# Opening a decoder layer with x0 loaded first, modulation per single input block, and sums of squares by column groups on TensorE

## The chip, the cores and the metric

The kernel runs on one core of one Trainium2 chip. The metric is device time in microseconds (us) of one execution, which covers the span of the profile and the little that lies around it. Smaller is better.

## What is computed

One inference step of a hybrid decoder layer for 1024 prompt tokens and 8 short sample sequences of 8 tokens (64 rows), model width 2048, all in float32. What matters here:

```python
def rmsnorm(x, g):
    xf = x.astype(jnp.float32)
    y = xf * lax.rsqrt(jnp.mean(xf * xf, axis=-1, keepdims=True) + EPS)
    return y.astype(x.dtype) * g
...
    mod = jax.nn.silu(c) @ w_ada + b_ada            # (9, 2048) @ (2048, 6144)
    shift, scale, gate = jnp.split(mod[:, None, :], 3, axis=-1)
    xn = rmsnorm(x, norm_g) * (1.0 + scale) + shift
    z = xn @ w_in                                    # 5120 columns
...                                                  # three mixers, two of them with a layernorm
    out = jnp.concatenate([ya, yb, yc], axis=-1) @ w_out
    return x + gate * out, ...                       # then a final rmsnorm
```

So before the first column of `z` can be summed over the 2048 input channels, the kernel needs the root mean square of every token (a sum over all channels) and, for each block of 128 channels, its shift and scale, which are two blocks of columns of a 2048-deep product with `w_ada`.

## The kernel before

Channels lie on the 128 partitions, tokens on the free axis. The width 2048 is 16 blocks of 128 (`KT` = 16). Tokens go through in two parts: T0 = 512 prompt tokens, then T1 = 576 (the other 512 and the 64 sample rows). Every large product is made of three matmuls: activations and weights are split into a high and a low part (`xn_hi`, `xn_lo`, `w_hi`, `w_lo`), and `mm3` (L131 to L133) adds hi·hi, hi·lo and lo·hi in PSUM. ScalarE makes `w_hi` (L97), VectorE makes `w_lo` (L98), per loaded weight tile.

The change concerns the **opening**, which is everything until the first product of T0 stands. It holds three kinds of work, all fed by DMAs that SyncE issues in one queue:
- the modulation: `w_ada` for shift and scale, 64 blocks of 512 KB, an odd block as one DMA into a tile of the pool tag `ar` (L689) and an even one as two DMAs of 256 KB into spare `xn_hi`/`xn_lo` tiles (L694). `ada_mm` (L142) multiplies with `silu(c)` (`cz`, 32 columns wide with padding), so that four such matmuls write four groups of 32 PSUM partitions. A **unit** in the kernel before is 8 blocks: four column blocks (shift and scale of two input blocks) over all of the depth. `ada_fin` copies the result to SBUF (ScalarE, `rows`, L168), transposes it on TensorE (L169) and adds bias and norm weight on VectorE into `adam` (L173, L178).
- the tokens: 16 loads of `x0` (L658), squares on ScalarE (L662, L665), two running sums `acc0` on VectorE (L666), then `rstd_of`: matmuls with a 128-column piece of the sum as weights and the one column of `one_d` as moving operand (`ps_var`, L210), a reciprocal square root with one Newton step on the few resulting columns (`rstd_cols`, L188 to L194), and `row_bcast` (`ps_bc`, L201), which spreads it over all partitions for R0 (L717).
- the first six column blocks of `w_in` (`ps_g`): `k_step(k)` loads `wi_g[k]` (384 KB, three buffers), splits it, and issues 6 x 3 matmuls of 512 columns. It needs `xn[k]` from `norm_x` (L225 to L227), and so `adam` of block k and R0.

The loop of the opening has nine turns: turn i multiplies unit i (8 blocks) and, one turn behind, runs `norm_pair(i - 1)` and two `k_step`s. Units 0 and 1 come before the first `k_step`, with all x0 loads in the middle of unit 0.

`rstd_of` and `row_bcast` are also used by the four layernorms, by the sums of squares of the second part's tokens (`stats_x1`), and by the three final normalisations, the last of which ends the kernel.

The code is written once in program order; a scheduler with priorities (`tc.high_priority`) then fixes the order of instructions on each engine, and each engine runs its list in that order.

Of the kernel before, what the change touches and what calls it, by code (L numbers as in the profile page):

```python
# [44 lines left out]
def decoder_layer(ctx: ExitStack, tc: tile.TileContext, a):  # L45
# [21 lines left out]
    with tc.high_priority(10 * HP):  # L67
        nc.sync.dma_start(cT, a["cT"])
# [817 lines left out]
```

## Time and profile before

| | us |
|---|---|
| median of three runs | 1513.63 (1512.84 to 1514.2) |
| the profiled execution | 1511.97 |
| its span in the profile | 1510.3 |
| opening, up to the first matmul of `ps_s` | 137.0 |
| TensorE busy in the span | 1469.2 (97%) |
| VectorE busy | 923.8 (61%) |
| ScalarE busy | 597.7 (40%) |

The rows below come from that one profiled execution, which lies 1.7 us under the median. PE is TensorE's matmul stream, PEld its weight loads, DVE is VectorE, ACT ScalarE, POOL GpSimd, SP SyncE. Starts are counted from the span's start. A float32 matmul appears as two instructions. Matmul durations overlap (the next one starts before the last has drained), so the pace of TensorE is read from starts. The idle time in brackets, with an arrow, tells what ended it.

### The profile page before, as it was taken

To read this page: it belongs to the slowest core of one execution; us is meant where nothing else is said; L and a number is where in the kernel's file an instruction comes from. 1 tells how busy PE (TensorE), PEld (TensorE's weight loads), DVE (VectorE), ACT (ScalarE), POOL (GpSimd) and SP (SyncE) were. 2 spreads that over 40 slices of the span, in tenths; PEclk is the share of its full clock that TensorE was granted. 3 is DMA by queue.
4 is the path that set the end of the run, shared out by engine and by line. 5 is a ranking of instruction groups with operands and counts; after the bars stand their busy time and mean duration, and the time that the engine had idled before them with its cause. 6 is when DMAs were issued, how large, how long until landed. Compare 5 with 4: busy or idle time off the path is not lost.

```text
span 1510.3 us, 25287 instructions
## 1 busy us (share of the span) xinstructions
PE 1469.2 (97%) x10072; PEld 1320.9 (87%) x10072; DVE 923.8 (61%) x1760; ACT 597.7 (40%) x1006; POOL 48.6 (3%) x120
## 2 busy tenths in 40 slices
PE   4999999999999999999999999999999999999996
PEld 3777888887777778888999999999999999999996
DVE  4436993679467452554885995387956744334345
ACT  4225422264557442433533422235445753222220
POOL 0000000010000000000000000011100000000000
PEclk9999999999999999999999999999999999999998
DMA  9995233334444543564573222222222221244323
GB/s 365 411 367 183 81 102 98 98 98 145 159 162 149 163 152 103 168 201 149 157 240 105 76 74 91 81 84 86 94 88 71 70 80 59 81 132 124 107 79 126
DMA packets 86550, 206.10 MB, mean 136 GB/s; under 512 B 10656, under 2 KB 26656, under 8 KB 86432
## 3 DMA queue, kind: packets, MB, share of 16 engines
q1 hardware_dynamic: 85280, 203.30, 41.3%
q8 instruction: 79, 1.29, 0.3%
q10 hardware_dynamic: 1152, 1.18, 0.2%
q14 instruction: 39, 0.32, 0.1%
HBM read 194.70 MB, written 9.74 MB: 135 GB/s over the span
## 4 chain that ended last, share of the span: by engine, by line
PE 92%; DMA 4%; DVE 2%; ACT 1%; issue 1%; SPq 0%; DVEq 0%; ACTq 0%
PE ps_s L131 23%; PE ps_s L132 23%; PE ps_s L133 22%; PE ps_g L133 6%; PE ps_g L131 6%; PE ps_g L132 6%; PE ps_ada L146 2%; DMA a_raw<-w_ada 2%; DMA w_raw<-wi_g 1%; PE ps_bc L201 1%; DMA x<-x 1%; PE ps_gate L131 1%; PE ps_var L210 1%; DVE w_lo L98 1%; PE ps_gate L132 0%
## 5 line engine op out<-in xcount | busy, mean ns | idle before, releaser
L98 DVE TENSOR_TENSOR w_lo<-w_raw,w_hi 128x512 fp32r<-128x512 f32 (+1 forms) x480 | 311.3, 653 | 407.6 <-PE ps_s L133 266.8
L131 PE MATMUL ps_s<-xn_hi,w_hi 128*128 128x288 f32 (+1 forms) x1632 | 538.4, 330 | 1.8 <-ACT pad_a L421 1.6
L97 ACT CAST w_hi<-w_raw 128x512 fp32r<-128x512 f32 (+1 forms) x480 | 281.4, 592 | 651.2 <-PE ps_s L132 451.8
L132 PE MATMUL ps_s<-xn_lo,w_hi 128*128 128x288 f32 (+1 forms) x1632 | 534.6, 328 | 0.0
L133 PE MATMUL ps_s<-xn_hi,w_lo 128*128 128x288 f32 (+1 forms) x1632 | 532.5, 326 | 0.0
L131 PEld LDWEIGHTS ps_s<-xn_hi,w_hi 128*128 128x128 f32 x1632 | 306.0, 188 | 28.4 <-issue 2.8
L133 PEld LDWEIGHTS ps_s<-xn_hi,w_lo 128*128 128x128 f32 x1632 | 307.1, 188 | 22.0 <-issue 0.2
L132 PEld LDWEIGHTS ps_s<-xn_lo,w_hi 128*128 128x128 f32 x1632 | 306.5, 188 | 20.6 <-issue 0.5
L358 DVE SCALAR_TENSOR_TENSOR mx<-pad_b,vec,mx 128x512 f32<-128x512 f32 x240 | 177.6, 746 | 2.4
L131 PE MATMUL ps_s<-m_hi,w_hi 128*128 128x288 f32 (+1 forms) x480 | 157.1, 327 | 0.0
L132 PE MATMUL ps_s<-m_lo,w_hi 128*128 128x288 f32 (+1 forms) x480 | 156.6, 326 | 0.0
L133 PE MATMUL ps_s<-m_hi,w_lo 128*128 128x288 f32 (+1 forms) x480 | 156.5, 326 | 0.0
L131 PE MATMUL ps_g<-xn_hi,w_hi 128*128 128x288 f32 (+1 forms) x288 | 95.4, 331 | 0.7
L133 PEld LDWEIGHTS ps_s<-m_hi,w_lo 128*128 128x128 f32 x480 | 90.3, 188 | 6.2
L132 PEld LDWEIGHTS ps_s<-m_lo,w_hi 128*128 128x128 f32 x480 | 90.1, 188 | 6.2
L131 PEld LDWEIGHTS ps_s<-m_hi,w_hi 128*128 128x128 f32 x480 | 90.0, 187 | 6.2
L133 PE MATMUL ps_g<-xn_hi,w_lo 128*128 128x288 f32 (+1 forms) x288 | 93.5, 329 | 1.7 <-DVE w_lo L98 1.7
L131 PE MATMUL ps_g<-m_hi,w_hi 128*128 128x288 f32 (+1 forms) x288 | 94.2, 328 | 0.1
L132 PE MATMUL ps_g<-xn_lo,w_hi 128*128 128x288 f32 (+1 forms) x288 | 94.1, 327 | 0.0
L132 PE MATMUL ps_g<-m_lo,w_hi 128*128 128x288 f32 (+1 forms) x288 | 93.9, 326 | 0.0
L133 PE MATMUL ps_g<-m_hi,w_lo 128*128 128x288 f32 (+1 forms) x288 | 93.6, 326 | 0.0
L133 PEld LDWEIGHTS ps_g<-xn_hi,w_lo 128*128 128x128 f32 x288 | 54.2, 188 | 8.3 <-DVE w_lo L98 4.7
(200 smaller groups left out, 1462.8 us busy)
## 6 DMA issues: line engine op xcount, KB each, us to landing
w_raw<-wi_s SPq DMA_DIRECT2D x136, 512.0 KB, 3.5
w_raw<-wo_s SPq DMA_DIRECT2D x40, 512.0 KB, 3.5
a_raw<-w_ada SPq DMA_DIRECT2D x64, 256.0 KB, 6.8
a_raw<-w_ada SPq DMA_DIRECT2D x32, 512.0 KB, 6.9
g_raw<-w_ada SPq DMA_DIRECT2D x64, 256.0 KB, 2.9
w_raw<-wi_g SPq DMA_DIRECT2D x16, 384.0 KB, 7.1
w_raw<-wo_g SPq DMA_DIRECT2D x16, 384.0 KB, 3.0
w_raw<-wi_g SPq DMA_DIRECT2D x32, 192.0 KB, 2.5
```

The lines of the kernel that those rows point to most:

```text
L97: nc.scalar.copy(hi, raw)
L98: nc.vector.tensor_tensor(lo, raw, hi.bitcast(F32), op=ALU.subtract)
L131: nc.tensor.matmul(out, wh, xh, start=start, stop=False)
L132: nc.tensor.matmul(out, wh, xl, start=False, stop=False)
L133: nc.tensor.matmul(out, wl, xh, start=False, stop=stop)
L146: nc.tensor.matmul(pa[32 * j:32 * j + 32, 0:P], cz[:, k, :], raw[q][:, j * P:(j + 1) * P], start=(k == 0), stop=(k == KT - 1))
L201: nc.tensor.matmul(pb[:, c * w:(c + 1) * w], st[0:w, 1, c0 + c:c0 + c + 1].to_broadcast([w, P]), ident[0:w, 0:w], start=True, stop=True)
L210: nc.tensor.matmul(pv[0:w, c:c + 1], s[:, u + c * w:u + (c + 1) * w], ones[:, 0:1], start=(s is src[0]), stop=(s is src[-1]))
L358: nc.vector.scalar_tensor_tensor(out[:, :T0], pad[:, j:j + T0], w[:, j:j + 1], out[:, :T0], op0=ALU.mult, op1=ALU.add)
```

## The change

x0 comes first: its 16 loads stand ahead of `w_ada` (with one half block and the first 64 columns of `vec` between them), and `cT` moves to ScalarE's DMA queue. A unit of modulation becomes four blocks for **one** input block: the four groups of 32 partitions now hold shift and scale for two halves of the depth, and `ada_fin` adds the halves on VectorE. The opening has 16 turns: modulation of block i+1, then `norm_x(i)` and `k_step(i)`. Sums of squares are no longer added up on VectorE for x0; `var_mm` lets four matmuls with a 32-column weight of ones write four partition groups, each a quarter of the tokens, so the reciprocal square root works on rows of a quarter of the tokens (128, 144 or 72 columns) on all partitions, and `row_bcast` picks one partition per group. That form replaces the old one everywhere. The rest of `vec` (columns 64 on), and what is worked out from `lam` (`sw`, `sp8`), comes after the opening.

```diff
-        nc.sync.dma_start(cT, a["cT"])
+        nc.scalar.dma_start(cT, a["cT"])
...
-    def ada_mm(pa, b, raw):
+    def ada_mm(pa, raws, b, fine):
         for q in range(2):
-            k = 2 * b + q
+            t = 2 * b + q
             for j in range(4):
-                nc.tensor.matmul(pa[32 * j:32 * j + 32, 0:P], cz[:, k, :], raw[q][:, j * P:(j + 1) * P],
-                                 start=(k == 0), stop=(k == KT - 1))
+                k = 2 * t + j // 2 if fine else t
+                nc.tensor.matmul(pa[32 * j:32 * j + 32, 0:P], cz[:, k, :], raws[q][:, j * P:(j + 1) * P],
+                                 start=(t == 0), stop=(t == (7 if fine else 15)))
...
+    def ada_fin(k, pa):
+        pt = ada_turn(pa)
         with tc.high_priority(HP):
...
+            nc.vector.tensor_tensor(dst, pt[:, 0:2, :],
+                                    vec[:, o:o + 2].unsqueeze(2).to_broadcast([P, 2, 9]), op=ALU.add)
+            nc.vector.tensor_tensor(dst, dst, pt[:, 2:4, :], op=ALU.add)
...
+            nc.vector.tensor_scalar(sc, sc, 1.0, vec[:, o:o + 1], op0=ALU.add, op1=ALU.mult)
...
-    def row_bcast(st, c0, n):
+    def row_bcast(st, w, j0, n):
         pb = mi("ps_bc")
-        w = 96 if n % P else P
-        for c in range(n // w):
-            nc.tensor.matmul(pb[:, c * w:(c + 1) * w], st[0:w, 1, c0 + c:c0 + c + 1].to_broadcast([w, P]),
-                             ident[0:w, 0:w], start=True, stop=True)
+        for j in range(n):
+            nc.tensor.matmul(pb[:, j * w:(j + 1) * w], ident[:, 32 * (j0 + j):32 * (j0 + j) + 1].to_broadcast([P, P]),
+                             st[:, 1, 0:w], start=True, stop=True)
         return pb
+
+    def var_mm(pv, s, u, w, ones, start, stop):
+        for j in range(4):
+            nc.tensor.matmul(pv[32 * j:32 * j + 32, 0:w], ones.to_broadcast([P, 32]), s[:, u + j * w:u + (j + 1) * w],
+                             start=start, stop=stop)
...
-            acc = acc0[k % 2]
-            if k < 2:
-                nc.scalar.activation(acc, x[:, :T0], AF.Square)
-            else:
-                sq = sp_.tile([P, TM], F32, tag="xr", name="x_sq")
-                nc.scalar.activation(sq[:, :T0], x[:, :T0], AF.Square)
-                nc.vector.tensor_tensor(acc, acc, sq[:, :T0], op=ALU.add)
...
+            sq = sp_.tile([P, TM], F32, tag="xr", name="x_sq")
+            nc.scalar.activation(sq[:, :T0], x[:, :T0], AF.Square)
+            var_mm(pv, sq, 0, P, one_d, k == 0, k == KT - 1)
...
+    for k in range(KT):
+        load_x0(k, pv0)
+        if k == 12:
+            with tc.high_priority(HP):
+                nc.sync.dma_start(vec[:, :64], a["vec"][:, :64])
+    with tc.high_priority(HP):
+        st0 = rstd_rows(pv0[:, 0:P], P)
+    for b in range(2):
+        ada_block(0, b)
+    with tc.high_priority(HP):
+        nc.scalar.copy(R0, row_bcast(st0, P, 0, 4))
+    for b in range(2, 4):
+        ada_block(0, b)
...
+    ada_fin(0, ada_ps[0])
+    for i in range(KT):
+        if i + 1 < KT:
+            for b in range(4):
+                ada_block(i + 1, b)
         with tc.high_priority(HP):
...
+            xn[i] = norm_x(i, x0[i], R0, T0)
+        k_step(i, (lambda: ada_fin(i + 1, ada_ps[i + 1])) if i + 1 < KT else None)
...
-    nc.sync.dma_start(vec[:, o:], a["vec"][:, o:])
+    nc.sync.dma_start(vec[:, 64:], a["vec"][:, 64:])
```

`k_step` calls `ada_fin` of the next block after its third column block. `ada_rows` (the copy to `rows`) is called at the end of each unit's fourth block. How the lists of the engines come out of this shows at three places.

TensorE's list in the middle of the opening, where one unit of modulation ends and a `k_step` begins; first before:

```order
L133 MATMUL ps_g<-xn_hi,w_lo 128x512
L146 MATMUL ps_ada<-a_raw,cz 32x128 x64
L169 MATMUL ps_ada<-ident,rows 128x128
L131 MATMUL ps_g<-xn_hi,w_hi 128x512
L132 MATMUL ps_g<-xn_lo,w_hi 128x512
L131 MATMUL ps_g<-xn_hi,w_hi 128x512
L132 MATMUL ps_g<-xn_lo,w_hi 128x512
L131 MATMUL ps_g<-xn_hi,w_hi 128x512
L133 MATMUL ps_g<-xn_hi,w_lo 128x512
```

and the same place in the changed kernel:

```order
L147 MATMUL ps_ada<-a_raw,cz 32x128 x32
L181 MATMUL ps_ada<-ident,rows 128x128
L131 MATMUL ps_g<-xn_hi,w_hi 128x512
L132 MATMUL ps_g<-xn_lo,w_hi 128x512
L131 MATMUL ps_g<-xn_hi,w_hi 128x512
L133 MATMUL ps_g<-xn_hi,w_lo 128x512
```

The transpose stands directly behind the unit's last matmul in both, ahead of all of the `k_step`'s matmuls. Before, 36 matmuls of `ps_g` follow until the next unit, and the first with `w_lo` is the sixth; now 18 follow, and it is the fourth.

ScalarE's list at the same place, before and then changed (`x_2_166` and `x0_1_121` are tiles of x0):

```order
L168 COPY rows<-ps_ada 128x128
L97 CAST w_hi<-w_raw 128x384 x4
L226 ACTIVATE xn_hi<-x_2_166,adam 128x512
L226 ACTIVATE xn_hi<-x_3_171,adam 128x512
L168 COPY rows<-ps_ada 128x128
```

```order
L177 COPY rows<-ps_ada 128x128
L97 CAST w_hi<-w_raw 128x384 x2
L244 ACTIVATE xn_hi<-x_1_121,adam 128x512
L177 COPY rows<-ps_ada 128x128
L97 CAST w_hi<-w_raw 128x384 x2
```

and VectorE's:

```order
L173 TENSOR_TENSOR adam<-ps_ada,vec 128x36
L178 SCALAR_TENSOR_TENSOR adam<-adam,vec 128x2x9
L225 SCALAR_TENSOR_TENSOR x_2_166<-x_2_166,adam,R_113 128x512
L98 TENSOR_TENSOR w_lo<-w_raw,w_hi 128x384 x4
L225 SCALAR_TENSOR_TENSOR x_3_171<-x_3_171,adam,R_113 128x512
```

```order
L189 TENSOR_TENSOR adam<-ps_ada,vec 128x18
L191 TENSOR_TENSOR adam<-adam,ps_ada 128x18
L194 TENSOR_SCALAR adam<-adam,vec 128x9
L98 TENSOR_TENSOR w_lo<-w_raw,w_hi 128x384 x2
L243 SCALAR_TENSOR_TENSOR x_1_121<-x_1_121,adam,R_111 128x512
L245 SCALAR_TENSOR_TENSOR xn_lo<-x_1_121,adam,xn_hi 128x512
```

On ScalarE the casts that make `w_hi` stay behind the copy to `rows`, now once per `k_step` and no longer once per two. On VectorE the first `w_lo` loses one large operation ahead of it and gets a third small one.

SyncE's queue where x0 ends and the first `wi_g` is reached, changed kernel (`x_15_234` is the last x0 tile):

```order
L677 DMA x_15_234<-x 128x512
L705 DMA a_raw<-w_ada 128x512
L701 DMA a_raw<-w_ada 128x1024
L705 DMA a_raw<-w_ada 128x512 x2
L701 DMA a_raw<-w_ada 128x1024
L705 DMA a_raw<-w_ada 128x512 x2
L701 DMA a_raw<-w_ada 128x1024
L705 DMA a_raw<-w_ada 128x512 x2
L701 DMA a_raw<-w_ada 128x1024
L104 DMA w_raw<-wi_g 128x768
```

Before, 16 blocks of `w_ada` stand ahead of the first `wi_g`; now there are eight (the half block that is missing here was issued behind the first x0).

## Rows read from the trace of the kernel before

**Rows 1.** The page: busy time of TensorE, and the gigabytes per second that the DMAs moved in 40 equal slices of the span (37.8 us each).

```profile
PE 1469.2 (97%) x10072; PEld 1320.9 (87%) x10072; DVE 923.8 (61%) x1760; ACT 597.7 (40%) x1006; POOL 48.6 (3%) x120
GB/s 365 411 367 183 81 102 98 98 98 145 159 162 149 163 152 103 168 201 149 157 240 105 76 74 91 81 84 86 94 88 71 70 80 59 81 132 124 107 79 126
```

**Rows 2.** Busy time in three stretches (start:end, length, then PE, PEld, DVE, ACT and POOL with their instructions, granted clock, DMA share, GB/s): until the `k_step`s, the `k_step`s, and the rest up to the last matmul of the large products.

```profile
0.00:39.00 39.00, 19.28 (x274) 13.23 (x274) 17.10 (x55) 17.01 (x29) 1.57 (x12) 1.00 0.98 367
39.00:137.00 98.00, 93.10 (x1063) 74.58 (x1063) 40.54 (x79) 29.01 (x60) 2.27 (x6) 1.00 0.92 351
137.00:1494.00 1357.00, 1354.21 (x8724) 1230.97 (x8723) 856.71 (x1600) 550.99 (x918) 44.76 (x103) 1.00 0.37 114
```

**Rows 3.** What TensorE waited for in the first 125 us: total us, times, longest.

```profile
PE ps_ada L146 <- DMA a_raw<-w_ada: 19.2, 7, 9.7
PE ps_ada L169 <- ACT rows L168: 3.1, 7, 0.5
```

**Rows 4.** DMA issues of the first 125 us: count, KB each, median us from issue to landing.

```profile
a_raw<-w_ada SPq DMA_DIRECT2D x32, 512.0 KB, 6.9
w_raw<-wi_g SPq DMA_DIRECT2D x16, 384.0 KB, 7.1
```

**Rows 5.** TensorE in order of time until the first `k_step`: start, us, instructions merged.

```profile
10.95 1.08 PE L146 MATMUL ps_ada<-a_raw,cz 128*32 128x128 f32 x16 [0.62 <-DMA a_raw<-w_ada]
...
22.91 0.65 PE L146 MATMUL ps_ada<-a_raw,cz 128*32 128x128 f32 x8 [9.69 <-DMA a_raw<-w_ada]
...
31.02 1.93 PE L146 MATMUL ps_ada<-a_raw,cz 128*32 128x128 f32 x32
...
34.88 3.37 PE L146 MATMUL ps_ada<-a_raw,cz 128*32 128x128 f32 x88
38.71 0.33 PE L169 MATMUL ps_ada<-ident,rows 128*128 128x128 f32 x1 [0.45 <-ACT rows L168]
```

**Rows 6.** One hand-over from a unit of modulation to its `k_step`s, all engines in order of time, to the same point of the next.

```profile
48.07 3.70 PE L146 MATMUL ps_ada<-a_raw,cz 128*32 128x128 f32 x128
...
51.89 0.27 ACT L168 COPY rows<-ps_ada 128x128 f32<-128x128 f32 x1 [8.32 <-PE ps_ada L146]
52.05 1.75 ACT L97 CAST w_hi<-w_raw 128x384 fp32r<-128x384 f32 x4
...
52.21 0.33 PE L169 MATMUL ps_ada<-ident,rows 128*128 128x128 f32 x1 [0.44 <-ACT rows L168]
...
52.57 0.20 DVE L173 TENSOR_TENSOR adam<-ps_ada,vec 128x36 f32<-128x36 f32 x1 [8.22 <-PE ps_ada L169]
...
52.62 0.50 PE L131 MATMUL ps_g<-xn_hi,w_hi 128*128 128x512 f32 x1
...
52.80 0.18 DVE L178 SCALAR_TENSOR_TENSOR adam<-adam,vec 128x18 f32<-128x18 f32 x1
...
53.02 0.75 DVE L225 SCALAR_TENSOR_TENSOR x<-x,adam,R 128x512 f32<-128x512 f32 x1
...
53.69 1.96 DVE L98 TENSOR_TENSOR w_lo<-w_raw,w_hi 128x384 fp32r<-128x384 f32 x4
...
54.29 0.50 PE L133 MATMUL ps_g<-xn_hi,w_lo 128*128 128x512 f32 x1 [0.24 <-DVE w_lo L98]
...
61.23 0.39 PE L133 MATMUL ps_g<-xn_hi,w_lo 128*128 128x512 f32 x1
61.55 1.19 PE L146 MATMUL ps_ada<-a_raw,cz 128*32 128x128 f32 x36
...
65.69 0.33 PE L169 MATMUL ps_ada<-ident,rows 128*128 128x128 f32 x1 [0.44 <-ACT rows L168]
```

**Rows 7.** TensorE at the end of the opening, in order of time.

```profile
135.65 0.39 PE L131 MATMUL ps_g<-xn_hi,w_hi 128*128 128x512 f32 x1
...
137.01 0.39 PE L131 MATMUL ps_s<-xn_hi,w_hi 128*128 128x512 f32 x1
```

**Rows 8.** Sums of squares and their spreading inside the stream of large matmuls: busy time of `ps_var`'s instructions in a stretch with one layernorm of T0 and in one with `stats_x1` of T1 (PE, PEld, DVE), then of `ps_bc`'s in the same stretches (PE, PEld, DVE, ACT), and one block of column-group matmuls (`ps_ada` of a gate) in the stream of a product.

```profile
140.00:170.00 30.00, 0.94 (x8) 1.04 (x8) 0.16 (x1) 1.00 0.29 96
700.00:720.00 20.00, 1.10 (x12) 1.17 (x12) 0.15 (x1) 1.00 0.34 105
...
140.00:170.00 30.00, 1.05 (x8) 1.04 (x8) 0.00 (x0) 0.59 (x1) 1.00 0.29 96
700.00:720.00 20.00, 1.58 (x12) 1.41 (x12) 0.00 (x0) 0.74 (x2) 1.00 0.34 105
...
366.98 0.64 PE L146 MATMUL ps_ada<-g_raw,cz 128*32 128x128 f32 x16
```

**Rows 9.** The end of the kernel in order of time, and, as the first row, the one reciprocal of 8 columns.

```profile
13.95 0.20 DVE L739 RECIPROCAL sw<-sw 128x8 f32<-128x8 f32 x1
...
1496.70 0.64 PE L210 MATMUL ps_var<-one_d,acc_y 128*96 128x1 f32 x6 [2.29 <-DVE acc_y L634]
1497.38 0.16 DVE L188 TENSOR_SCALAR st<-ps_var 96x3 f32<-96x3 f32 x1 [0.82 <-PE ps_var L210]
...
1497.81 0.17 DVE L190 RECIPROCAL st<-st 96x3 f32<-96x3 f32 x1 [0.27 <-ACT st L189]
...
1498.90 1.57 PE L201 MATMUL ps_bc<-ident,st 96*128 96x96 f32 x6 [1.56 <-DVE st L194]
```

More of the change, by code (lines that the diff above doesn't have):

```diff
@@ L38 @@
 OUT_K = [12, 13, 14, 15, 0, 1, 2, 3, 4, 5, 6, 8, 9, 10, 11, 7]
-ADA = [16 * (j % 2) + 2 * u + j // 2 for u in range(8) for j in range(4)] + list(range(32, 48))
+ADA = [16 * (j % 2) + k for k in range(16) for j in range(2)] + list(range(32, 48))
 N_GRP = 6
@@ L216, in rstd_tile @@
         st = rstd_of([src], 0, T, ones)
[L217 to L218 removed]
+        hs = halves(T)
+        for h, (u, v) in enumerate(hs):
+            n = 4 // len(hs)
+            nc.scalar.copy(R[:, u:v], row_bcast(st, T // 4, h * n, n)[:, :v - u])
         return R
@@ L652, in decoder_layer, with load_x0 @@
     x0 = []
-    acc0 = [ap.tile([P, T0], F32, tag=f"acc{i}", name="acc0", bufs=1) for i in range(2)]
-    def load_x0(k):
+    xn = {}
+    gt = []
+    def load_x0(k, pv):
         with tc.high_priority(HP):
@@ L678, in k_step, with ada_load @@
                     xh, xl, T0, k == 0, k == KT - 1)
+            if c == 2 and turn:
+                turn()
     ada_ps = {}
[L682 to L684 removed]
+    def ada_load(f):
         with tc.high_priority(HP):
[L686 to L687 removed]
+            src = a["w_ada"][f]
+            if f % 2:
                 big = ap.tile([P, 1024], F32, tag="ar", name="a_raw")
                 nc.sync.dma_start(big, src)
[L690 to L695 removed]
@@ L697, in decoder_layer @@
-    R0 = ap.tile([P, T0], F32, tag="R0", name="R0", bufs=1)
-    o = VEC["h0"][0]
-    def norm_pair(i):
-        with tc.high_priority(HP):
-            for q in range(2 * i, 2 * i + 2):
-                xn[q] = norm_x(q, x0[q], R0, T0)
-    for i in range(9):
-        if i < 8:
-            for b in range(8):
-                ada_block(i, b)
-                if i == 0 and b == 3:
-                    with tc.high_priority(HP):
-                        nc.sync.dma_start(vec[:, :o], a["vec"][:, :o])
-                    for k in range(KT):
-                        load_x0(k)
-        if i == 1:
-            with tc.high_priority(HP):
-                nc.vector.tensor_tensor(acc0[0], acc0[0], acc0[1], op=ALU.add)
-                st = rstd_of([acc0[0]], 0, T0, one_d)
-                nc.scalar.copy(R0, row_bcast(st, 0, T0))
-            gt.extend(pmm.tile([P, 2, 512], F32, tag="mm", name="ps_g") for _ in range(3))
-        if i > 0:
-            norm_pair(i - 1)
-            k_step(2 * (i - 1))
-        if i < 8:
-            ada_fin(i, ada_ps[i])
-        if i > 0:
-            k_step(2 * (i - 1) + 1)
+                return [big[:, :512], big[:, 512:]]
@@ new lines, in ada_load, with ada_block @@
+            raw = [xp.tile([P, TM], F32, tag=t, name="a_raw") for t in ("xh", "xl")]
+            for q in range(2):
+                nc.sync.dma_start(raw[q][:, :512], src[:, q * 512:(q + 1) * 512])
+            return raw
+    def ada_block(k, b):
+        if b == 0:
+            ada_ps[k] = mi("ps_ada")
+        ada_mm(ada_ps[k], ada_load(4 * k + b), b, True)
+        if b == 3:
+            ada_rows(ada_ps[k])
+    R0 = ap.tile([P, T0], F32, tag="R0", name="R0", bufs=1)
+    pv0 = mi("ps_var")
@@ new lines, in decoder_layer @@
+    for k in range(KT):
[7 more added lines that the diff above has]
+        ada_block(0, b)
+    with tc.high_priority(HP):
+        nc.scalar.copy(R0, row_bcast(st0, P, 0, 4))
+    for b in range(2, 4):
+        ada_block(0, b)
+    gt.extend(pmm.tile([P, 2, 512], F32, tag="mm", name="ps_g") for _ in range(3))
```

80 lines of the change are left out of this document (34 added, 46 removed).

## Prediction

> **What bounds the kernel now.** I read the page first: TensorE is busy 97% of the span, so whatever moves the time has to pass through its stream [rows 1]. Then the busy time by stretch: from 137 us on TensorE is busy 1354.2 of 1357.0 us, which leaves no holes to close there, only work to shorten; until 39 us it is busy half of the time; and between 39 and 137 us, where the `k_step`s run, 4.9 of 98 us are open even by its modelled ends [rows 2]. The second to third numbers of the DMA line (411, 367 GB/s) show that loads run at full pace through the opening's middle [rows 1]. The waits say which of the two binds: TensorE waits 19.2 us for blocks of `w_ada`, and the long pieces of that stand ahead of the first `k_step` (9.7 us alone while x0 passes, the row at 22.91) [rows 3, 5]. After 39 us it is another pattern: from one transpose to the next takes 65.69 - 52.21 = 13.48 us, and no wait for a DMA stands in it [rows 6]. Loads for such a turn are 8 blocks of 512 KB and two of 384 KB [rows 4], 4.98 MB, 12.1 us at 411 GB/s. So the opening has a beginning that waits for loads and then a TensorE-paced part with a fixed loss in every turn.
>
> **Where the 13.48 us of a turn go** [rows 6]. From the start of the unit's matmuls (48.07) to the copy `rows` (51.89) 3.82; to the transpose 0.32; to VectorE's first small operation (52.57) 0.36; to the first `w_lo` (53.69) 1.12; to the first matmul with `w_lo` (54.29) 0.60; and from there, with 31 of the 36 matmuls, to the next unit (61.55) 7.26. The reader should see a relay: the transpose waits for ScalarE's copy, the first `ps_g` matmul (52.62) for `w_hi`, which ScalarE casts only behind that copy, and the sixth for `w_lo`, which VectorE makes only behind the small operations and one `x`. Each runner is idle for long and is late only because its work stands behind another's in the list. The weights themselves had landed.
>
> **The change, its start.** With x0 and eight blocks ahead of the first `wi_g`, and no longer x0 and 16 blocks, the first `k_step` can begin earlier. The half block that arrived at 22.91 [rows 5] had behind it 16 tiles of x0 (4.19 MB), five blocks (2.62) and 0.22 of small tensors, 7.03 MB. In the changed kernel the last block of unit 1 has 4.19 + 4.19 + 0.11 = 8.50 MB; 1.47 MB more at 0.411 MB/us is 3.6 us, so it lands at 26.5 us. Its 16 instructions take 1.08 us (the row at 10.95), then 0.12 to the copy and 0.32 to the transpose: 28.0 us, where before it is 38.71 [rows 5]. That is a head start of 10.7 us. x0's last tile lands, by the same line, at 16.9 us, which leaves 11 us for R0 and the first `norm_x`; I count nothing for it (bounds 0 and 1 us).
>
> **The change, its turns.** A turn is now four blocks and one `k_step`, and the order of the lists shows the same relay once per turn: `rows`, the transpose directly behind the unit, `w_hi` behind `rows`, `w_lo` behind VectorE's small operations. Link by link: the unit has 64 instructions fewer, at (3.70 - 1.19)/(128 - 36) = 0.0273 each [rows 6], so 3.82 - 1.75 = 2.07. 0.32 and 0.36 stay. Ahead of `w_lo` there are three small operations at 0.22 (52.80 to 53.02) instead of two and an `x`: 0.67. 0.60 stays. Then 15 matmuls follow instead of 31 (the first with `w_lo` is the fourth of 18), at (137.01 - 135.65)/6 = 0.227 [rows 7]: 7.26 - 3.63 = 3.63. Sum 7.65 us per turn, 15.3 for two, where 13.48 did. Loads of a turn are 2.49 MB, 6.1 us, so they don't bind. From the transpose of unit 1 there are 14 turns: 28.0 + 107.1 = 135.1. Then 0.36 + 0.67 + 0.60 and 15 + 18 matmuls (7.5): the first `ps_s` at 144.2, where before it is 137.0 [rows 7]. The head start is eaten by sixteen relays in place of eight: **+7.2 us**. Bounds: if the third small operation and the PSUM read cost nothing, 0.2 less per turn (-3); if `w_lo` is late by as much as before, 0.45 more (+6).
>
> **Clock at the start.** 32 instructions in 1.93 us (31.02) against 128 in 3.70 (48.07) show the array at half pace until the row at 34.88, whose 88 in 3.37 are a mixture [rows 5, 6]: the lower of its two levels (1.2 GHz), though the granted clock is printed as 1.00 for that stretch [rows 2]. Before it rose, the array had run x0's sums and some 200 instructions of units since 22.91. The changed kernel feeds it from the first square of x0 on and has done more than that by 28 us, so the rise is likely past or near; bounds 0 and 5.8 us (one whole turn's 1.75 + 4.1 at half pace). I take **+1.0**. The Trainium skill, page "TensorE: Matmul & The Clock Gate", section "What's actually happening", says that an array that was idle starts at 1.2 GHz and gets 2.4 only after sustained work; by that rule the array could still be at 1.2 GHz when the first turn begins, and the sum would take the upper bound.
>
> **The rest of the kernel.** VectorE loses x0's 14 additions and gets wider reciprocal roots; in the stream TensorE has the following. Sum of squares: 8 instructions by column groups instead of 8 or 12 with a full weight load. The nearest row is a block of 16 column-group instructions in 0.64 us [rows 8]; eight fewer make 0.42, and 0.09 is lost ahead of such a block (61.23 to 61.55 is 0.32, not 0.227 [rows 6]): 0.51 against 0.94 (T0) and 1.10 (T1). Spreading: T0 unchanged; T1 8 instructions instead of 12, 1.05 against 1.58. Three places in T0 (two layernorms, y0) give 3 x 0.43, three in T1 3 x 1.12; the first final half has two `ps_bc` more (0.26). **-4.4 us** (bounds 0, if the time there is VectorE's, and -6). The late `vec` and 20 small operations on `lam` fall into T0's first products; VectorE is busy 857 of 1357 us there [rows 2], and the `w_lo` tiles are made ahead, so 0; without that cover some 4 us, 20 at 0.2.
>
> **The end.** After the last matmul nothing covers the chain [rows 9]. Five small operations get 72 columns instead of 3; by the rows at 52.57 (36 columns, 0.20) and 1497.38 (0.16) a column costs 0.0012, so 5 x 0.08; the reciprocal by 0.20 at 8 columns and 0.17 at 3 costs 0.006 a column, 0.4 (rounded rows; from 0 up); the root 0.1; two more `ps_bc` of 1.57/6 each 0.5; `ps_var` -0.1. **+1.3 us**. The Trainium skill's page "VectorE: DVE Perf Modes", section "First, the fixed hardware budget", says that the divide of a reciprocal repeats eight times per element; by that the 72 columns would take 0.6 us in place of 0.4, and the sum would be 0.2 more; no row has a wide reciprocal.
>
> **Sum.** 7.2 + 1.0 - 4.4 + 1.3 = +5.1 us on the profiled 1511.97, 1517.1. That execution lies 1.7 under the median of the runs shown, so against the median 1513.63 it is 1518.7.
>
> **Rivals.**
> - *The relay is shorter than its parts* (no measurable change). If ScalarE's cast or VectorE's first `w_lo` comes half a microsecond earlier because less stands ahead of it, a turn is about 7.3, and the sum falls by 14 x 0.35: 1513.8. For it: `w_lo` loses the large operation ahead of it. Against: the fourth matmul comes earlier too, and the cast is still behind the copy. The total is zero at 7.29 per turn.
> - *The relay is hidden* (faster). The code puts the transpose behind the third column block; were it to run there, the copy and the cast would lie under matmuls and the loads would set the pace: 6.1 per turn, 14 x 1.55 = 21.7 less, 1497. For it: only 12.1 of 13.48 us are loads' time. Against: TensorE's list has the transpose directly behind the unit. It is faster by 0.2% from 7.07 us per turn down.
> - *The low clock lasts into the turns*, with R0 late as well: 5.8 and 1 instead of 1.0, 1524.5. For it: until 28 us the array again follows the loads; against: the work that it has then done, above.
> - That the opening simply gains its head start (10.7 us, 1503) is excluded by the count of relays, unless the second rival holds.
>
> **How the numbers follow.** Forecast (1515.7 to 1522) 0.60, shorter relay 0.20, hidden relay 0.09, low clock 0.11. 0.2%, 3 us, is about what a measurement of this kernel can tell from no change. Slower is the forecast and the low clock, 0.71; same 0.20; faster 0.09. The range takes in the shorter relay and most of the low clock: 1512 to 1524.
>
> **What would show it.** 16 transposes, the second at 28 us, then 7.65 us apart, each behind a wait for `rows` and with waits for `w_hi` and `w_lo` behind it; the first `ps_s` at 144 to 145 us; `ps_var` in T1 at half a microsecond; the last stretch, from `acc_y` on, 1.3 us longer. I am wrong if the transposes lie under 7.3 us apart, if TensorE waits for DMAs between them, or if `ps_var` or `w_lo` waits appear after 145 us.

## The result, and the profile after

The changed kernel takes 1525.4 us (1524.7 to 1527.3) where the kernel before, on the same chip, takes 1513.2: a ratio of 1.0088, 95% interval 1.0076 to 1.0100. That is slower, and more so than the 1512 to 1524 us forecast. The profiled execution's span is 1525.6 us, 15.3 over the 1510.3 of before. The profiled one is the slowest of the changed kernel's four executions and that of before the fastest of its four, so of these 15.3 us the medians show 12.2.

First the page of the changed kernel (engines, then granted clock in tenths by slices of 38.1 us), which answers to [rows 1]:

```profile
PE 1480.7 (97%) x10184; PEld 1316.9 (86%) x10184; DVE 931.0 (61%) x1777; ACT 600.9 (39%) x1014; POOL 47.8 (3%) x120
...
PEclk8999999999999999999999999999999999999998
```

TensorE is as full as before, so again only the stretches tell something. Cut at the first `ps_g` (29.6 us), at the first `ps_s`, at 200 us and ahead of the end (columns as in [rows 2]):

```profile
0.00:29.60 29.60, 18.53 (x266) 10.11 (x266) 5.02 (x14) 15.46 (x26) 1.46 (x12) 0.83 0.95 349
29.60:144.30 114.70, 105.03 (x1198) 77.44 (x1199) 47.42 (x112) 31.41 (x68) 0.60 (x4) 1.00 0.87 318
144.30:200.00 55.70, 51.05 (x243) 40.71 (x242) 49.30 (x111) 26.31 (x43) 2.90 (x6) 0.94 0.34 113
200.00:1509.00 1309.00, 1303.81 (x8463) 1186.64 (x8462) 819.34 (x1519) 527.05 (x877) 42.81 (x98) 1.00 0.36 115
```

The third row is the new thing. TensorE is open for 4.65 of 55.7 us, and its mean clock there is 0.94. Before, as many us from the first `ps_s` on had hardly a hole:

```profile
137.00:192.70 55.70, 55.57 (x278) 45.28 (x277) 53.77 (x97) 25.93 (x45) 1.31 (x5) 1.00 0.29 88
```

To see where the 15.3 us arise, I put each `ps_s` and `ps_g` matmul of one trace beside the same one of the other and followed the distance between their starts: 7.3 us at the first `ps_s` (144.32 against the 137.01 of [rows 7]), 15.15 us from about 200 us on, 13.84 us at 1474, and 15.3 at the end. So the opening gives +7.3, the first layernorm of T0 +7.9, all the rest of the stream -1.3, the end +1.5.

**One turn of the opening**, all engines in order of time, answers to [rows 6]:

```profile
28.87 0.27 ACT L177 COPY rows<-ps_ada 128x128 f32<-128x128 f32 x1 [0.57 <-PE ps_ada L147]
...
29.19 0.33 PE L181 MATMUL ps_ada<-ident,rows 128*128 128x128 f32 x1 [0.44 <-ACT rows L177]
29.55 0.18 DVE L189 TENSOR_TENSOR adam<-ps_ada,vec 128x18 f32<-128x18 f32 x1 [0.47 <-PE ps_ada L181]
...
30.12 1.02 DVE L98 TENSOR_TENSOR w_lo<-w_raw,w_hi 128x384 fp32r<-128x384 f32 x2
...
30.72 0.50 PE L133 MATMUL ps_g<-xn_hi,w_lo 128*128 128x512 f32 x1
...
34.35 1.95 PE L147 MATMUL ps_ada<-a_raw,cz 128*32 128x128 f32 x64
...
36.75 0.33 PE L181 MATMUL ps_ada<-ident,rows 128*128 128x128 f32 x1 [0.44 <-ACT rows L177]
```

The same relay as before, now once per `k_step`: copy, transpose 0.32 later, the first `w_lo` 0.93 behind the transpose, the first matmul with it 0.60 later. A turn is 36.75 - 29.19 = 7.56 us, and all 14 lie between 7.54 and 7.60.

**The first layernorm of T0.** SyncE issues the late `vec`, VectorE waits for it, and TensorE waits for VectorE:

```profile
143.03 0.43 SPq L741 DMA_DIRECT2D vec<-vec  x1
...
147.30 0.69 DVE L98 TENSOR_TENSOR w_lo<-w_raw,w_hi 128x512 fp32r<-128x512 f32 x1 [0.78 <-PE ps_s L133]
...
150.56 0.17 DVE L748 TENSOR_SCALAR sw<-vec 128x8 f32<-128x8 f32 x1 [2.56 <-DMA vec<-vec]
150.64 0.55 DVE L374 TENSOR_SCALAR mx<-pad_b,vec 128x512 f32<-128x512 f32 x1
...
151.78 0.69 DVE L307 TENSOR_TENSOR ln_s<-ln_s,mx 128x512 f32<-128x512 f32 x1
...
152.62 1.10 PE L310 MATMUL ps_mean<-ln_s,one_c 128*128 128x512 f32 x2 [1.10 <-DVE ln_s L307]
```

The reader should see one queue holding up two: the operation that needs `vec` (L748) is only a small one, but `ln_s` (L307), which needs nothing from `vec`, stands behind it on VectorE, and `ps_mean` on TensorE stands behind that. VectorE never catches up, because from here to 190 us it is busy for nearly all of the time. Windows of TensorE's stream, with the granted clock behind the busy times:

```profile
180.00:185.00 5.00, 4.63 (x26) 3.36 (x25) 4.76 (x11) 1.61 (x3) 0.00 (x0) 1.00 0.09 26
185.00:190.00 5.00, 2.82 (x20) 2.20 (x19) 4.78 (x10) 0.99 (x2) 0.00 (x0) 1.00 0.40 133
190.00:195.00 5.00, 4.23 (x19) 3.47 (x18) 4.13 (x9) 3.17 (x5) 0.00 (x0) 0.50 0.00 0
195.00:200.00 5.00, 5.00 (x22) 4.31 (x22) 4.23 (x9) 1.21 (x3) 0.21 (x1) 0.82 0.08 26
```

and what TensorE waited for from 144 to 200 us:

```profile
PE ps_mix L131 <- ACT tok_h L337: 1.4, 2, 0.7
PE ps_mix L133 <- DVE tok_l L338: 1.2, 2, 0.8
PE ps_mean L310 <- DVE ln_s L307: 1.1, 1, 1.1
PE ps_tr L336 <- DVE mx L357: 0.7, 1, 0.7
...
```

Counted in the trace, 144 `ps_s` matmuls (three column blocks of 48, as many as the pool of their accumulators has buffers) lie between 144.32 and 184.0, and no more until 196.04. Before, the chain from `ps_mean` to the last `ps_mix` ended at 180.3, when 140 of these had been started and four were left, 0.9 us of work. The chain had no more slack than that, and one that ends later runs bare: transpose, ScalarE's copy, VectorE's `tok_l` and `ps_mix` take turns, TensorE is open for 2.2 of 5 us from 185 on, and then its clock is granted at 0.50. From 194.12 to 196.04 nine `ps_mix` take 0.213 us each where they take 0.119 at 185; adding up such differences from 190.0 to 197.1 gives some 2.3 us. Whether the clock falls there in every execution is not shown: its mean over the span is 0.990 in the profiled one and 0.993 to 0.995 in the other three.

The slack can be checked with the traces of the first three experiments below. From the first `ps_s` to the last `ps_mix` of this layernorm it takes 43.2 us before, 43.9 and 44.0 in experiments 1 and 3, 47.3 in experiment 2 and 51.5 in the changed kernel. Between the first `ps_s` and 200 us the stream loses, in the same order, 0.0, 0.0 and -0.2, 3.2, and 7.8 us. A chain that is 0.8 us longer costs nothing, and a longer one nearly all of its excess.

**The sums** (`ps_var`, then `ps_bc`, answers to [rows 8]):

```profile
155.00:185.00 30.00, 0.42 (x8) 0.18 (x8) 0.28 (x1) 1.00 0.28 85
715.00:735.00 20.00, 0.45 (x8) 0.16 (x8) 0.30 (x1) 1.00 0.38 108
...
155.00:185.00 30.00, 1.10 (x8) 0.97 (x8) 0.00 (x0) 0.59 (x1) 1.00 0.28 85
715.00:740.00 25.00, 1.25 (x8) 1.03 (x8) 0.00 (x0) 0.80 (x2) 1.00 0.33 94
```

**The end** answers to [rows 9]:

```profile
1510.51 0.33 PE L220 MATMUL ps_var<-acc_y,one_d 128*32 128x72 f32 x8 [2.29 <-DVE acc_y L652]
1510.90 0.23 DVE L202 TENSOR_SCALAR st<-ps_var 128x72 f32<-128x72 f32 x1 [0.54 <-PE ps_var L220]
...
1511.52 0.60 DVE L204 RECIPROCAL st<-st 128x72 f32<-128x72 f32 x1 [0.39 <-ACT st L203]
...
1513.31 1.95 PE L214 MATMUL ps_bc<-st,ident 128*128 128x72 f32 x8 [2.46 <-DVE st L208]
```

From the start of `ps_var` to that of `ps_bc` it is 2.80 us, before 2.20; `ps_bc` takes 0.38 more.

### The profile page after: what moved, and what is told of

It reads as the page before. It is cut to its first block, busy times and chain, and to the rows that moved or that the text cites. A ratio compares the mean times of both kernels' runs of the same rounds, so it can differ in the third digit from the quotient of the medians.

```text
span 1525.6 us, 25535 instructions
## 1 busy us (share of the span) xinstructions
PE 1480.7 (97%) x10184; PEld 1316.9 (86%) x10184; DVE 931.0 (61%) x1777; ACT 600.9 (39%) x1014; POOL 47.8 (3%) x120
## 4 chain that ended last, share of the span: by engine, by line
PE 89%; DVE 5%; DMA 3%; issue 1%; ACT 1%; SPq 0%; DVEq 0%; ACTq 0%
PE ps_s L131 22%; PE ps_s L132 22%; PE ps_s L133 22%; PE ps_g L133 6%; PE ps_g L132 5%; PE ps_g L131 5%; PE ps_ada L147 3%; DMA a_raw<-w_ada 1%; DVE w_lo L98 1%; DMA x<-x 1%; PE ps_bc L214 1%; PE ps_gate L131 1%; PE ps_gate L132 0%; DMA vec<-vec 0%; DMA w_raw<-wi_g 0%
```

## Experiments

**1. `vec` early again in the changed kernel.**

```diff
-                nc.sync.dma_start(vec[:, :64], a["vec"][:, :64])
+                nc.sync.dma_start(vec[:, :VEC["h0"][0]], a["vec"][:, :VEC["h0"][0]])
...
-    nc.sync.dma_start(vec[:, 64:], a["vec"][:, 64:])
+    nc.sync.dma_start(vec[:, VEC["h0"][0]:], a["vec"][:, VEC["h0"][0]:])
```

`VEC["h0"][0]` is 288; in the kernel before, `o` has this value.

> The changed kernel with 288 columns of `vec` loaded early, as before the change, in place of 64; nothing else. Theory A (the late `vec` holds up VectorE: 2.56 us of waiting at 148 us and 20 small operations in a stretch in which VectorE has no room, and from there the holes in TensorE's stream and the half clock after 184 us): the shift between the two kernels no longer grows from 7.3 to 15.2 us between 144 and 200 us but stays under 9, no ps_mean, ps_tr or ps_mix wait over 0.3 us there, granted clock 1.00 throughout; 1517 to 1519 us. Theory B (the wider reciprocal root, six operations on 128 columns instead of 4, is what VectorE has no room for): the holes stay, 1523 to 1525.5 us.

Measured: 1518.5 us, ratio to the kernel before 1.0040 (1.0026 to 1.0055), so 7.3 us (0.0048 of 1512, with some 2 us of interval on either ratio) under the changed kernel. The stretch from its first `ps_s` (142.6) to 200 us:

```profile
142.60:200.00 57.40, 57.27 (x286) 45.64 (x285) 55.82 (x99) 26.91 (x45) 3.23 (x6) 1.00 0.36 120
```

TensorE is full, the clock 1.00, and the distance to the kernel before, 5.56 us at the first `ps_s`, is 5.53 from 182 us until beyond 450 us. The wider reciprocal root is still in this kernel. Theory A holds; B falls. The edit also moves the start: the second transpose comes at 27.66 us in place of 29.19, so the first `ps_s` is 1.75 us earlier. The two traces lie 10.0 us apart, 7.9 of them from this layernorm; the changed kernel's lies 1.9 us above its median, this one 1.0 below.

**2. Only the late `vec`, in the kernel before.**

```diff
-                        nc.sync.dma_start(vec[:, :o], a["vec"][:, :o])
+                        nc.sync.dma_start(vec[:, :64], a["vec"][:, :64])
...
-    nc.sync.dma_start(vec[:, o:], a["vec"][:, o:])
+    nc.sync.dma_start(vec[:, 64:], a["vec"][:, 64:])
```

> The kernel before with only the load of `vec` cut as in the change: 64 columns early, 1440 late. Theory A1 (the late load is dear by where it stands: here it is issued at about 127 us, 10 us ahead of the first `ps_s`, lands 8 us later and nothing waits; only the 20 small operations remain, at 0.08 to 0.1 us of VectorE's time each): 1513 to 1516 us. Theory A2 (the 20 operations in a full VectorE are enough to open holes): 1517 to 1521 us.

Measured: 1515.3 us, ratio 1.0025 (1.0016 to 1.0034), +3.8 us; in the trace +3.7, of which 3.4 arise between 136 and 182 us. The load and its wait in order of time, then TensorE's waits from 137 to 200 us:

```profile
127.24 0.43 SPq L728 DMA_DIRECT2D vec<-vec  x1
...
135.38 0.17 DVE L735 TENSOR_SCALAR sw<-vec 128x8 f32<-128x8 f32 x1 [1.20 <-DMA vec<-vec]
```

```profile
PE ps_mix L133 <- DVE tok_l L320: 1.0, 1, 1.0
PE ps_mix L131 <- ACT tok_h L319: 0.7, 1, 0.7
PE ps_mean L292 <- DVE ln_s L289: 0.6, 1, 0.6
```

The time fits A1, its mechanism only in part: there is a wait, 1.20 us, and TensorE's holes are those of the changed kernel in small. The late load and the operations that need it therefore cost about 4 us even where it is issued 10 us ahead of the first `ps_s`. No run has one without the other, but the trace tells their sizes. The wait ends at 135.38, 2.1 us ahead of the first `ps_s`. The small operations on `lam` (26 in the trace, not 20) come behind it, one by one between the large ones, and hold VectorE for 4.3 us, from the start of each to that of the operation behind it; `ps_mean` starts 8.6 us behind the first `ps_s` where it was 4.5. In the changed kernel the load is issued 1.3 us ahead of the first `ps_s` and waited for twice as long (2.56), and the same 26 operations hold VectorE for 2.0 us.

**3. Only the new sums, in the kernel before** (`var_mm`, `rstd_rows` and the spreading in all places; x0's two running sums stay).

```diff
-        w = 96 if n % P else P
-        for c in range(n // w):
-            for s in src:
-                nc.tensor.matmul(pv[0:w, c:c + 1], s[:, u + c * w:u + (c + 1) * w], ones[:, 0:1],
-                                 start=(s is src[0]), stop=(s is src[-1]))
-        return rstd_cols(pv[0:w, 0:n // w], w, n // w)
+        w = n // 4
+        for s in src:
+            var_mm(pv, s, u, w, ones, s is src[0], s is src[-1])
+        return rstd_rows(pv[:, 0:w], w)
```

> The kernel before with only the new sums: `ps_var` by column groups, `rstd_rows`, and the spreading from them, x0's opening as before. My term was -4.4 us in the stream and +1.3 at the end: 1510 us. The trace of the changed kernel shows the shift fall by only 1.3 us from 200 us on and grow by 1.5 at the end: 1513 to 1514 us by that. If the wider reciprocal root is what VectorE has no room for at 150 to 190 us (theory B): 1515 to 1520 us.

Measured: 1513.9 us, ratio 1.0012 (1.0003 to 1.0022), +1.8 us. By distance to the kernel before: +3.1 at the first `ps_s`, then 2.9 falls to 1.8 by 1315 us, and the end adds 1.7. That makes 3.5 us in the trace, where the profiled execution lies 1.6 us above the median of the runs. So no layernorm of this kernel turned the sums into holes, and my -4.4 is -1.1. The +3.1 was not expected. R0's chain of 128-column operations is not covered in that opening: TensorE waits 1.7 us for the root and then 1.6 us for the first `w_hi`, and the granted clock is 0.50 from 40.9 to 44.4 us, where `ps_g` matmuls start 0.43 us apart. Two rows of the chain in order of time:

```profile
31.35 0.95 DVE L190 RECIPROCAL st<-st 128x128 f32<-128x128 f32 x1 [0.38 <-ACT st L189]
...
33.69 1.13 PE L200 MATMUL ps_bc<-st,ident 128*128 128x128 f32 x8 [1.68 <-DVE st L194]
```

**4. `wi_g` one step ahead in the changed kernel.**

```diff
-    def k_step(k, turn):
-        hl = load_w(a["wi_g"][k], N_GRP * P, 2)
+    def k_step(k, turn, hl):
...
+        hl_next = load_w(a["wi_g"][i + 1], N_GRP * P, 2) if i + 1 < KT else None
-        k_step(i, (lambda: ada_fin(i + 1, ada_ps[i + 1])) if i + 1 < KT else None)
+        k_step(i, (lambda: ada_fin(i + 1, ada_ps[i + 1])) if i + 1 < KT else None, hl)
+        hl = hl_next
```

> The changed kernel with each `wi_g` row loaded and cast one `k_step` ahead, nothing else; TensorE's list then has `ps_g` matmuls between the blocks of a unit and around the transpose. If the relay (copy, transpose, small operations, cast, `w_lo`) is what makes a turn 7.57 us, a turn falls to the sum of TensorE's work, about 32 at 0.027 to 0.065 and 18 at 0.227, 6.2 us (or to the loads' 6.1), and the first `ps_s` starts near 124 us: 1503 to 1507 us with the late `vec` still in it. If something else sets the turn (ScalarE, VectorE or the loads at their real pace), the turn stays over 7.2 and the time over 1519 us.

Measured: 1541.3 us, ratio 1.0184 (1.0166 to 1.0201): the opposite. A turn is 7.9 and 8.9 us in alternation, and the first `ps_s` starts at 161.5. TensorE's waits from 28 to 160 us, then one hand-over:

```profile
PE ps_g L131 <- ACT xn_hi L244: 14.6, 16, 2.0
```

```profile
95.10 0.28 PE L181 MATMUL ps_ada<-ident,rows 128*128 128x128 f32 x1
...
96.65 0.23 DVE L194 TENSOR_SCALAR adam<-adam,vec 128x9 f32<-128x9 f32 x1
...
97.70 0.72 ACT L244 ACTIVATE xn_hi<-x,adam 128x512 fp32r<-128x512 f32 x1 [1.89 <-DVE x L243]
...
98.47 0.50 PE L131 MATMUL ps_g<-xn_hi,w_hi 128*128 128x512 f32 x1 [0.71 <-ACT xn_hi L244]
...
98.91 0.43 PE L147 MATMUL ps_ada<-a_raw,cz 128*32 128x128 f32 x8
...
99.26 0.50 PE L132 MATMUL ps_g<-xn_lo,w_hi 128*128 128x512 f32 x1
...
99.60 0.40 PE L133 MATMUL ps_g<-xn_hi,w_lo 128*128 128x512 f32 x1
```

Two things took the relay's place. The transpose now stands in the middle of a `k_step`, so the hand-over that remains (transpose to `xn_hi` to `ps_g`, 98.47 - 95.10 = 3.37 us) is bare at its end, 0.7 to 0.9 us per turn. And the unit stands in pieces among the large matmuls. From 98.91 to 99.60 it is 0.69 for a piece of 8 and one `ps_g`, where 8 at 0.027 and 0.23 make 0.45; with the 0.10 lost at the piece's front (0.327 from a `ps_g` to a piece, for 0.227), one piece costs 0.3 us beyond its work. The two turns have four and five pieces. My sum of a turn was wrong besides: it took a unit's 32 matmuls as 0.9 us, but the profile has two instructions for each, 64 at 0.027, 1.75 us (34.35 above). TensorE's own work in a turn is 18 at 0.227, 1.75 and the transpose's 0.35, 6.2 us, before any piece. The expectations of the next runs carry the same error where they say 0.9.

**5. Each unit two `k_step`s ahead** (from here to experiment 9 `vec` is early as in the first). The edit is shown against the kernel of experiment 4.

```diff
     for i in range(KT):
-        if i + 1 < KT:
+        if i + 2 < KT:
             for b in range(4):
-                ada_block(i + 1, b)
-        with tc.high_priority(HP):
-            xn[i] = norm_x(i, x0[i], R0, T0)
+                ada_block(i + 2, b)
+        if i + 1 < KT:
+            with tc.high_priority(HP):
+                xn[i + 1] = norm_x(i + 1, x0[i + 1], R0, T0)
...
```

> The kernel with 288 columns of `vec` early and `wi_g` cast one step ahead, and besides each modulation unit two `k_step`s ahead of its use, so that the chain from the transpose to `xn_hi` (3.37 us in the kernel with `wi_g` ahead) has a whole turn to run under. TensorE's list has the 32 matmuls of a unit in six pieces among the 18 `ps_g`. Theory (a turn is the chain of hand-overs as long as it isn't covered, then TensorE's own work): no wait for `xn_hi`; a turn is 18 at 0.227, the unit at 0.9, the transpose 0.35 and about 0.3 us for each of six changes between column groups and full matmuls, 7.1 us, so some 0.45 us under the changed kernel's 7.57; 1509 to 1513 us. If interleaving costs nothing: 6.2 us, 1498 to 1502.

Measured: 1538.1 us, ratio 1.0170 (1.0155 to 1.0185), 25 us over what was expected. The waits for `xn_hi` are gone but for one (1.1 us), as expected, and a turn is 8.95 us with six pieces: 6.2 and six times 0.3 make 8.0, the transpose's wait for `rows` 0.4 more (5.3 us in 12 turns), and half a microsecond stays unexplained. Interleaving in six pieces is dearer than the relay that it hides.

**6 and 7. The unit's matmuls behind the `k_step`**, 56 of its 64 instructions in one piece, and the same with the old form in the last two halves.

```diff
-            if c == 2 and turn:
+            if c == 0 and turn:
...
+        raws = [ada_load(4 * (i + 2) + b) for b in range(4)] if i + 2 < KT else None
...
+                ada_mm(ada_ps[i + 2], raws[b], b, True)
+            ada_rows(ada_ps[i + 2])
```

and, in 7 alone, with the functions of the kernel before under the names `rstd_of_c` and `row_bcast_c`:

```diff
-                    pb = row_bcast(rstd_of([acc], u, v - u, one_d), (v - u) // 4, 0, 4)
+                    pb = row_bcast_c(rstd_of_c([acc], u, v - u, one_d), 0, v - u)
```

> As the one before, but the units are only one step ahead and their matmuls are written behind the `k_step`, the transpose behind its first column block: TensorE's list has 28 of the 32 in one piece, four behind the seventh `ps_g` after the transpose, and eleven `ps_g` between the transpose and the first use of the next `xn_hi`. The chain from the transpose to `xn_hi` is 3.0 to 3.4 us against 2.9 of cover, so a wait of 0 to 0.5; a turn is 18 at 0.227, 0.9, 0.35, two changes at 0.3 and that wait, 6.0 to 6.5 us, where the loads (2.49 MB at 398 GB/s) take 6.25: 1499 to 1506 us. If the hand-overs are not what made the turn long, it stays at 7.5 and 1517 to 1519 us.

> As the one before, with the sums of the two last halves in the column form of the kernel before; all else with the new sums. The chain from `acc_y` to the end of `ps_bc` after the last matmul took 4.39 us before and 5.38 after: 1.0 us less than the kernel without this, and up to 0.5 in the first of the two halves, which lies under other work, the other way. If the end's longer time was that of the outputs alone: the same time.

Measured: 1525.1 us, ratio 1.0079 (1.0063 to 1.0094), and 1524.1, 1.0073 (1.0057 to 1.0090). The first misses: a turn is 7.50 us, TensorE's 6.2, two pieces at 0.3 and a wait of 0.7. The view from 28 to 140 us:

```profile
PE ps_g L131 <- ACT xn_hi L244: 12.1, 13, 3.0
```

With the 3.0 us at the start left out, that is 0.7 to 0.8 for each turn. The two times do not tell the two ends apart. Their traces do: from the last `acc_y` to the end of `ps_bc` it is 5.30 and 4.70 us.

**8 and 9. One `k_step` further ahead still**, the unit in two pieces as in 6, against which the edit is shown; 9 also has the old end, by the edit of 7.

```diff
-        raws = [ada_load(4 * (i + 2) + b) for b in range(4)] if i + 2 < KT else None
+        raws = [ada_load(4 * (i + 3) + b) for b in range(4)] if i + 3 < KT else None
...
-        k_step(i, (lambda: ada_fin(i + 1, ada_ps[i + 1])) if i + 1 < KT else None, hl)
+        k_step(i, (lambda: ada_fin(i + 2, ada_ps[i + 2])) if i + 2 < KT else None, hl)
```

> As the kernel with the units behind the `k_step`, but each unit another `k_step` ahead, so that `xn_hi` has a whole turn more, with 28 matmuls of a unit still in one piece and four apart. That kernel waited 0.95 us per turn for `xn_hi` (12.1 us in 13 turns) and its turn was 7.50. Theory: that wait goes and nothing takes its place: 18 at 0.231, the unit at 0.9, the transpose 0.35 with up to 0.2 of waiting for its copy, two changes at 0.32, 6.3 to 6.6 us per turn, about the loads' 6.25; the first `ps_s` 12 to 15 us earlier than there (147.8): 1508 to 1514 us. If a turn is bound by a queue of loads that waits for buffers, or the hand-over moves on to another operation: 7.2 us or more, 1520 to 1526 us.

> As the one before, with the sums of the two last halves in the column form of the kernel before: 0.9 us less than that, by the same step between the two kernels of the earlier call (1525.08 and 1524.14).

Measured: 1517.1 us, ratio 1.0027 (1.0014 to 1.0040), and 1516.3, 1.0025 (1.0015 to 1.0034); the first misses its 1508 to 1514, and the two are not told apart. A turn is 6.94 us and TensorE has no hole in it:

```profile
60.00:100.00 40.00, 39.96 (x478) 28.40 (x480) 17.55 (x42) 10.25 (x22) 0.00 (x0) 1.00 1.03 391
```

That is 6.2 and two pieces, with 0.1 over, so a turn without a bare hand-over costs TensorE's own work, as the theory says. But the gain over 7.56 is mostly lost at the start, where the transposes of units 1 and 2 come at 37.6 and 49.1 us (29.19 and 36.75 in the changed kernel): the first `ps_s` is at 144.0, 1.4 us behind the first experiment's. Between 24 and 53 us TensorE waits 4.8 us for `xn_hi` and 1.0 for `w_hi`, and the granted clock is 0.50 from 27.4 to 34.2 and from 41.0 to 44.5 us.

**10 and 11. The same idea on the kernel before**: units for two `k_step`s, old sums, `vec` as there; `wi_g` cast one step ahead, unit u+2 written behind the `k_step`s of unit u. 11 has, besides, the new sums of experiment 3 where they are covered (layernorms, `acc_x`, y0).

```diff
+    for u in range(8):
+        h1 = k_load(2 * u + 1)
+        raws = [ada_load(u + 2, b) for b in range(4)] if u < 6 else None
+        k_step(2 * u, h0, (lambda: ada_fin(u + 1, ada_ps[u + 1])) if u < 7 else None)
+        h0 = k_load(2 * u + 2)
...
+        if u < 7:
+            norm_pair(u + 1)
+        k_step(2 * u + 1, h1)
+        if u < 6:
             for b in range(8):
...
+                ada_block(u + 2, b, raws[b])
```

> The kernel before (units for two `k_step`s, its own sums, `vec` as there) with only the turn rewritten: `wi_g` cast one step ahead, the unit's matmuls written behind the two `k_step`s, the transpose behind the first column block. TensorE's list has 36 and 28 matmuls of a unit in two pieces, five `ps_g` between the unit and the transpose and 23 `ps_g` and 36 matmuls from there to the first use of the next `xn_hi`. Theory (what a turn costs over TensorE's own work is the uncovered chain of hand-overs): 36 at 0.231, the unit 3.5, the transpose 0.35, two changes at 0.32, 12.8 us where it was 13.48, and the loads need 12.5; seven turns, 4 to 5 us less: 1507 to 1509 us. If turns of two were already at their bound (loads at their real pace): the same time as before, 1511 to 1514.

> As the one before, with the new sums in the layernorms, `acc_x` and y0, and the old ones for x0 and the two last halves. Alone, the new sums cost 3.1 us in the opening and about 1.5 at the end and gave back 1.1 between 200 us and the end; without the first two: 1.0 us less than the kernel without them. If the wider operations cost VectorE more than they save where it is full (150 to 190 us): the same or up to 1 us more.

Measured: 1506.5 us, ratio 0.9966 (0.9952 to 0.9981), and 1506.6, 0.9968 (0.9958 to 0.9979). A turn falls from 13.48 to 12.53 us and the first `ps_s` comes at 130.8. From 39 us to there, against the second row of [rows 2]:

```profile
39.00:131.00 92.00, 91.75 (x1063) 73.57 (x1062) 40.88 (x77) 28.97 (x58) 1.08 (x5) 1.00 0.97 373
```

The same 1063 instructions in 92 us where they took 98. This kernel beats both. The new sums add nothing to it that can be measured, where 1.0 us less was expected; in the traces of the two kernels they gain 1.0 us between the first `ps_s` and the end of the stream, and 0.5 us of later start and 0.6 at the end take that back.

## Why the prediction was wrong

- **The late `vec`: the step that failed.** The prediction said that the late `vec` and the 20 small operations "fall into T0's first products", that VectorE is busy 857 of 1357 us there, that "the `w_lo` tiles are made ahead, so 0". It is 7.3 us (experiment 1). Three errors lie in it. The 857 of 1357 is a mean over the whole stream; from 150 us on VectorE is 90 to 100% busy in each ten us until 190, and before as well (95 to 99% from 140 to 200). The cover was sought for `w_lo`, but the hand-over that ran out was the layernorm's, whose cover of three column blocks had 0.9 us left. And a load's wait was not priced at all: it was issued 1.3 us ahead of the first `ps_s`, behind other loads, and landed 7.5 us later. The fallback in the same sentence, "without that cover some 4 us, 20 at 0.2", is near what experiment 2 measured (3.8), where the operations hold VectorE for 4.3 us; there the price was right. In the changed kernel the layernorm ends 8.3 us later, seen from the first `ps_s`. The wait of 2.6, the operations' 2.0, the low clock's 2.3, and the 0.7 by which experiment 1 is late without any of them make 7.6; the other 0.7 was not traced.
- **The opening: right.** The second transpose at 29.19 us (28.0 forecast), a turn of 7.56 (7.65), the last transpose at 135.17 (135.1), the first `ps_s` at 144.32 (144.2). The two small misses cancel. The relay was shown by covering it: 6.94 against 7.56 per single turn, 12.53 against 13.48 per double one. That the head start is eaten by sixteen relays in place of eight holds.
- **The clock at the start: near in size, by another cause.** Unit 1 came 1.2 us late, where the term was +1.0, but that is luck. Its last block landed at 28.06 us in place of 26.5; TensorE waited 0.57 us for it, and its matmuls then ran at the full clock, which had been back since 26.1. In experiment 1 the same block landed at 26.54 and the transpose came at 27.66, though there the array ran at half pace until 19.5 us. The 1.2 are part of the opening's +7.3, so opening and clock together were forecast at 8.2. The rival with a low clock forecast 1524.5, near the result, but by another mechanism: no turn ran at 1.2 GHz.
- **The sums: right per place, wrong in sum.** -4.4 was forecast, -1.3 is in the stream (-1.1 in experiment 3), so this term was mis-sized by 3 us. A `ps_var` place costs TensorE 0.54 to 0.70 us from the matmul ahead of it to the one behind it where nothing waits, less their usual pace 0.35 to 0.5, close to the 0.51 assumed; but a place cost less before than I had it (0.94 to 1.19 with that pace still in it). Part of what was saved is given back where the wider root is waited for: y0's spreading waits 0.7 us for `st` where it waited 0.2. Where the rest goes was not traced.
- **The end: right within the scatter.** +1.3 forecast, +1.0 in the chain (4.39 to 5.38 us) and 0.5 behind it, in the outputs' landing, that I can't explain: it is there with the old end too (experiments 7, 9 and 11), and not in 10, which has none of the new sums. The chain itself scatters: with the old end it took 4.4 to 4.9 us in five traces, with the new one 5.3 to 5.5 in five, so the step is 0.4 to 1.1. The reciprocal was the uncertain part: 0.17 at 3 columns, 0.60 at 72 and 0.95 at 128, so 0.006 a column as estimated from rows. The Trainium skill, page "VectorE: DVE Perf Modes", section "First, the fixed hardware budget", has the divide repeat eight times per element, from which I had estimated 0.6 us for the 72 columns; the trace gives 0.43 over the 3 columns of before, so by the rows, not by that estimate.

Put together from the trace: 7.3 + 7.9 - 1.3 + 1.5 = 15.4 of 15.3 us, where 8.2 + 0 - 4.4 + 1.3 = 5.1 was forecast.

## What to carry to other kernels

A wait on an in-order engine is priced by what stands behind it in the list, and its cover by the busy time of that very stretch and by the end of the cover there (here three accumulators), never by a mean over the kernel. A constant that an engine needs early belongs ahead of the bulk loads; here 224 more columns of `vec` there were worth 7 us. And where a relay of small hand-overs paces a loop, start the next round's inputs a full round ahead and keep the small matmuls in one block: covering the relay by scattering them cost more than the relay.

## What was not expected of the hardware

- Each piece of column-group matmuls between full ones costs TensorE about 0.3 us beyond its instructions, whatever its length (8 or 56): 0.10 ahead of it, and 0.2 behind it. With six pieces a turn was 8.95 us, with two 6.94.
- The clock fell after gaps that were short, as the granted clock and the length of single instructions show together. A stretch ahead of a trace's first clock record is printed as 1.00 whatever the pace, so the 0.83 of the changed kernel's first row above is too high. There the sums of x0 take 0.42 us an instruction until 12.2 us, 0.27 to 0.30 from 12.7 to 15.6, and 0.42 again from 16.1. The records say 1.00 (2.4 GHz) from 12.5 us, 0.50 (1.2 GHz) from 15.9 and 1.00 from 26.1. Between rise and fall the sums ran as blocks of 0.43 us with 0.25 of idle time between them:

```profile
14.73 0.42 PE L220 MATMUL ps_var<-x_sq,one_d 128*32 128x128 f32 x8 [0.26 <-ACT x_sq L680]
15.40 0.42 PE L220 MATMUL ps_var<-x_sq,one_d 128*32 128x128 f32 x8 [0.24 <-ACT x_sq L680]
16.07 2.01 PE L220 MATMUL ps_var<-x_sq,one_d 128*32 128x128 f32 x24 [0.26 <-ACT x_sq L680]
```

  In experiment 1 the same sums ran at the lower level without such gaps, 60 instructions in one block of 5.19 us; the first record is 1.00 at 19.5 us, and the clock stays there until the end of the stream. At 190 us of the changed kernel it fell to 0.50 after five microseconds in which TensorE was busy for 2.8 and no gap was longer than 0.83. The Trainium skill, page "TensorE: Matmul & The Clock Gate", section "What's actually happening", says that an array must be kept at work to get 2.4 GHz; these stretches agree with it.
